# First mixer of a two-layer encoder: output products grouped by kind with the two heads alternating, and one diagonal product for both directions

## The chip, the core and the metric

The kernel runs on one core of one Trainium2 chip. Its time is device time in microseconds from the first to the last instruction with what lies around them, the median of three runs. The core has five engines with queues of their own: TensorE (PE in the profile, with PEld for its weight loads), VectorE (DVE), ScalarE (ACT), GpSimd (POOL) and SyncE (SP), which here issues DMAs. They wait for each other by semaphores.

## What is computed

An encoder trunk over 512 positions of 1024 channels: two mixers, each followed by a gated MLP with a width-3 convolution, and norms. The change lies in the first mixer, which holds four heads of gated linear attention (GLA) and four of HGRN2, all with 64 key and 128 value channels, forward and backward. Cut to that part, the reference is:

```python
def chunk_gated_scan(q, k, v, log_a, chunk):
    ...
    cum = jnp.cumsum(log_a, axis=3)
    rel = cum[:, :, :, :, None, :] - cum[:, :, :, None, :, :]
    decay = jnp.where(lower, jnp.exp(jnp.where(lower, rel, 0.0)), 0.0)
    scores = jnp.einsum('bhnid,bhnjd,bhnijd->bhnij', q, k, decay)
    o_intra = jnp.einsum('bhnij,bhnjv->bhniv', scores, v)
    ...                       # state carried from chunk to chunk
    o_inter = jnp.einsum('bhnid,bhndv->bhniv', q_in, prev)
    return (o_intra + o_inter).reshape(b, h, s, dv)

def bidir_scan(q, k_f, k_b, v, la_f, la_b, chunk):
    fwd = chunk_gated_scan(q, k_f, v, la_f, chunk)
    bwd = chunk_gated_scan(flip(q), flip(k_b), flip(v), flip(la_b), chunk)
    return fwd + flip(bwd)
```

A position meets itself in both directions with decay 1, so its diagonal score is q·k_f + q·k_b. In GLA both directions have the same k; in HGRN2 each has its own.

## The kernel before

The eight heads are worked in four pairs: 0 and 1 are GLA, 2 and 3 HGRN2. For pair p the tiles q, k and a (decays) hold head 0 in partitions 0 to 63 and head 1 in 64 to 127, the forward direction in columns 0 to 511 and the backward one behind it.

**Scores** (`scores`, from line 553). The scores inside a block of 128 positions are built over levels h = 1, 2, 4, ..., 64, and a first step h = 0 for the diagonal. `products(h)` issues small fp32 products in tile sc, a 64x64 quarter of TensorE's array each: head e chooses the rows of the array and one half of sc, position half b the columns. For h = 0 there are 32, both directions summed in place; ScalarE then copies the sum to s (L596). For h = 1 to 32 there are 32 each, of which VectorE takes what a mask allows into s (the mask copy, L610), for h = 64 there are 16, which ScalarE copies to A, the finished scores. Between levels VectorE multiplies decays into q and k (L602) and shrinks the decays (L606). A block of these products is a row of 32 or 64 records in the trace, since an fp32 product makes two records.

**Outputs** (`attend`, from line 639). TensorE transposes k (tile kT, copied by ScalarE, L654), multiplies it with v to the state changes dS, VectorE chains them to states Si (L666, L668), and TensorE forms the output of each head over four blocks J of 128 positions: A times v (kind A: 128 rows of the array), plus q times the state of each direction that has one (kind Q: 64 rows). The old order is head by head, block by block: A, Q; A, Q, Q; A, Q, Q; A, Q. Then each head is normalised (a square on ScalarE, a sum and a product on VectorE, a power on GpSimd), transposed (oT) and gated by the silu of p_g (L711).

**What fills TensorE between these**: the projections, which are 24 products of 512 columns each: p_q, p_k, p_hq, p_hz, v, the gates p_g0 to p_g7, and at the end wo. Their weights come by DMA and are split into two parts by ScalarE (L181) and VectorE (L183); a split waits until an older buffer of four is free.

**Order.** TensorE's order is set by a planner (class Sched): projections run as jobs in a list, and chains (scores, outputs) are resumed when a count of planned nanoseconds has passed. The count rises with each product by `cost` or by a formula on its size; the pauses stand in the table W (`lv0`, `o0` and so on). TensorE runs that order as it is; the orders of the other engines are made by a scheduler from it. PSUM tiles with tag hd have three buffers, which kT, dS and the outputs share.

Of the kernel before, what the change touches and what calls it, by code (L numbers as in the profile page):

```python
# [14 lines left out]
AF = mybir.ActivationFunctionType  # L15
ALU = mybir.AluOpType
PSUM = bass.MemoryType.PSUM

S = 512
# [116 lines left out]
class Net:  # L136
# [261 lines left out]
    def even(self):  # L398
# [16 lines left out]
        def et(shape, tag, name, bufs, dt=F32):  # L415
            return ep.tile(shape, dt, tag=tag, name=name, bufs=bufs)
# [4 lines left out]
        def hd_ps(shape, name):  # L421
            return pe.tile(shape, F32, tag="hd", name=name, bufs=3)
# [132 lines left out]
        def scores(p):  # L555
            yield (lambda: p < 2 or p - 2 in att), 0.0
            q, k, a = P[p]
            t = em.tile([128, S + 8], F32, tag=f"t{p % 2}", name=f"t{p}", bufs=1)
            s = et([128, 2, 256], f"s{p % 2}", f"s{p}", 1)
            s4 = s.rearrange("p e (J c) -> p e J c", c=64)  # L560
            A = et([128, 2, 4, 128], "A", f"A{p}", 2)

            def products(h):

                half = 256 * (next(turn) % 2)
                ps = two[:, :, half : half + 256].rearrange("p e (J c) -> p e J c", c=64)
                for J in range(4):
                    for d in range(2):  # L570
                        for b in range(2):
                            for e in range(2):
                                r = slice(64 * e, 64 * e + 64)
                                o = S * d + 128 * J + 64 * b
                                out = ps[64 * b : 64 * b + 64, e, J, :]
                                st, w = k[r, o : o + 64], q[r, o : o + 64]
                                if h == 64:
                                    if b == d:
                                        o += 64 - 128 * d
                                        self.mm(out, st, q[r, o : o + 64], cost=60)  # L580
                                elif h == 0:
                                    self.mm(out, st, w, d == 0, d == 1, cost=50)
                                else:
                                    half = lambda v: v.rearrange(
                                        "p (n two h) -> p n two h", two=2, h=h)[:, :, 1 - d, :]
                                    self.mm(half(out), st, half(w), cost=25)
                return ps

            psd = products(0)
            V.tensor_tensor(out=q, in0=q, in1=a[:, 0:S2], op=ALU.mult)  # L590
            T, h = a, 1
            while h <= 64:
                nb = S // h
                n = nb // 2
                if h == 1:
                    nc.scalar.activation(s, psd.rearrange("p e J c -> p e (J c)"), AF.Copy)  # L596
                yield W[f"lv{p}_0"] if h == 1 else W[f"lv{p}"]
                ps = products(h)
                for x, half, tt in (
                        (right_left(q, nb, h), right_left, left_right(T, nb, 1)),  # L600
                        (left_right(k, nb, h), left_right, right_left(T, nb, 1))):
                    V.tensor_tensor(  # L602
                        out=x, in0=x, in1=tt.to_broadcast([128, 2, n, h]), op=ALU.mult)
                nT = (t if h in (1, 4, 16) else a) if h < 64 else self.stile([128, 8], "t128", f"t128_{p}", 2)
                t2 = T[:, 0 : 4 * n].rearrange("p (n two) -> p n two", two=2)
                V.tensor_tensor(out=nT[:, 0 : 2 * n], in0=t2[:, :, 0], in1=t2[:, :, 1], op=ALU.mult)  # L606
                l, r = slice(0, 64), slice(64, 128)
                if h <= 32:
                    i = LV.index(h)
                    V.copy_predicated(  # L610
                        out=s4, mask=masks[:, i : i + 1, :].unsqueeze(1).to_broadcast([128, 2, 4, 64]),
                        data=ps)
                else:
                    nc.scalar.activation(A[l, :, :, r], ps[l], AF.Copy)
                    nc.scalar.activation(A[r, :, :, l], ps[r], AF.Copy)
                if h == 32:
                    nc.scalar.activation(A[l, :, :, l], s4[l], AF.Copy)
                    nc.scalar.activation(A[r, :, :, r], s4[r], AF.Copy)
                T = nT
                h *= 2  # L620
            AS[p] = (A, T)
            self.sch.chain(attend(p), W[f"at{p}"])
# [15 lines left out]
        def attend(p):  # L638
            g = p // 2
            yield (lambda: (g, 3) in VV), 0.0  # L640
            A, T = AS[p]
            Q, K = (dirs(x) for x in P[p][0:2])
            hv = [slice(128 * (u % 4), 128 * (u % 4) + 128) for u in (2 * p, 2 * p + 1)]
            heads = [slice(64 * e, 64 * e + 64) for e in range(2)]
            steps = ((0, 1, 2), (3, 2, 1))
            kTs, Sis = [], []
            for d in range(2):
                pk = hd_ps([128, 4, 128], f"kT{p}{d}")
                for J in steps[d]:
                    nc.tensor.transpose(pk[:, J, :], K[:, d, 128 * J : 128 * J + 128], self.ident)  # L650
                    self.sch.now += 107
                kT = et([128, 4, 128], "kT", f"kT{p}{d}", 2)
                c = slice(d, d + 3)
                nc.scalar.activation(kT[:, c], pk[:, c], AF.Copy)  # L654
                kTs.append(kT)
            yield W[f"dS{p}"]
            for d in range(2):
                dS = hd_ps([128, 4, 128], f"dS{p}{d}")
                for J in steps[d]:
                    for e in range(2):  # L660
                        self.mm(dS[heads[e], J, :], kTs[d][:, J, heads[e]], VV[g, J][:, hv[e]])

                Si = et([128, 4, 128], "Si", f"Si{p}{d}", 2)
                up = 1 - 2 * d
                c = steps[d][0]
                V.tensor_copy(Si[:, c + up, :], dS[:, c, :])  # L666
                for c in steps[d][1:]:
                    V.scalar_tensor_tensor(  # L668
                        out=Si[:, c + up, :], in0=Si[:, c, :], scalar=T[:, 4 * d + c : 4 * d + c + 1],
                        in1=dS[:, c, :], op0=ALU.mult, op1=ALU.add)  # L670
                Sis.append(Si)
            yield (lambda: p == 0 or (2 * p - 1 in fin and 2 * p - 2 in fin)), W[f"o{p}"]
            rest = []
            for e in range(2):
                u = 2 * p + e
                ps = hd_ps([128, 4, 128], f"o{u}")
                for J in range(4):
                    c = slice(128 * J, 128 * J + 128)
                    self.mm(ps[:, J, :], A[:, e, J, :], VV[g, J][:, hv[e]], True, False)
                    ds = [d for d in range(2) if J != 3 * d]  # L680
                    for d in ds:
                        self.mm(ps[:, J, :], Q[heads[e], d, c], Sis[d][heads[e], J, :], False, d == ds[-1])
                sq = self.actp.tile([128, 4, 128], F32, tag="nsq", name=f"osq{u}", bufs=2)
                nc.scalar.activation(sq, ps, AF.Square)
                ss = self.stile([128, 4], "ss", f"ss{u}", 2)
                V.tensor_reduce(out=ss, in_=sq, axis=mybir.AxisListType.X, op=ALU.add)
                col = self.rstd(ss, 128, 4, f"o{u}")
                o = et([128, 4, 128], "o", f"o{u}", 2)
                V.tensor_tensor(
                    out=o, in0=ps, in1=col.unsqueeze(2).to_broadcast([128, 4, 128]), op=ALU.mult)  # L690
                rest.append((u, o))
            att.add(p)
            for u, o in rest:
                yield W[f"cs{p}"]
                pt = sm_ps(f"oT{u}")
                for J in range(4):
                    nc.tensor.transpose(pt[:, 128 * J : 128 * J + 128], o[:, J, :], self.ident)
                    self.sch.now += 109
                o = o.rearrange("p a b -> p (a b)")
                if u not in RG:  # L700
                    nc.scalar.activation(o, pt, AF.Copy)
                    pt = o
                O[u] = (pt, o)
                finish(u)
# [902 lines left out]
```

## Time and profile before

| | |
|---|---|
| median of three runs | 1289.49 us (1288.77 to 1289.98) |
| profiled execution: its own time | 1288.18 us |
| its span, first to last instruction | 1286.2 us |
| TensorE, matmuls busy | 1258.7 us (98%) |
| VectorE busy | 836.5 us (65%) |
| ScalarE busy | 489.9 us (38%) |
| GpSimd busy | 189.8 us (15%) |
| mean granted TensorE clock | 0.993 of full speed |

Busy times are sums over the whole span. A matmul's record lasts longer than its share of the array, since the next one begins before it ends; the distance from start to start is what it costs. Times in rows count from the span's start.

### The profile page before, as it was taken

Reading aid. Unit: us, or ns where it says so; the run is one execution under the profiler, and the core shown is the slowest. Engines: PE = TensorE matmul, PEld = TensorE weight load, DVE = VectorE, ACT = ScalarE, POOL = GpSimd, SP = SyncE. Lnnn points to the kernel's source line nnn. Section 1 sums busy time; section 2 is a strip of 40 time slices with the busy share of each in tenths; the row PEclk is TensorE's granted clock in tenths of the full one; section 3 lists DMA queues with packets and bytes.
Section 4 is the critical chain, followed back from the end, with each engine's and each line's share of the span. In section 5 each row is a group of like instructions: output and inputs, shape, how many; then the busy total and the mean of one; then the engine's idle time right before and its main releaser. Section 6 shows DMA issues by size and latency. Waiting matters only on the chain. (4 is left out here: it accounts for less than half of the span.)

```text
span 1286.2 us, 19499 instructions
## 1 busy us (share of the span) xinstructions
PE 1258.7 (98%) x7863; PEld 1038.7 (81%) x7863; DVE 836.5 (65%) x1317; ACT 489.9 (38%) x657; POOL 189.8 (15%) x283
## 2 busy tenths in 40 slices
PE   7989999999999999999999999999999999999997
PEld 5767887888888888888888889788888888888887
DVE  6665277656999478637665885775577637755753
ACT  4523344333443244324442324333444314433442
POOL 2000000024008526230021330001200000000012
PEclk8999999999999999999999999999999999999999
DMA  7111321132332534333246532423232322233211
GB/s 227 55 51 50 108 83 58 51 99 99 99 99 69 168 102 129 115 124 110 87 160 227 175 100 76 148 82 99 99 99 99 98 96 91 85 106 98 90 58 67
DMA packets 53819, 132.95 MB, mean 103 GB/s; under 512 B 12193, under 2 KB 17505, under 8 KB 53729
## 3 DMA queue, kind: packets, MB, share of 16 engines
q1 hardware_dynamic: 53008, 131.15, 31.6%
q8 instruction: 62, 1.02, 0.3%
q10 hardware_dynamic: 720, 0.55, 0.1%
q14 instruction: 29, 0.23, 0.1%
HBM read 120.14 MB, written 11.53 MB: 102 GB/s over the span
## 5 line engine op out<-in xcount | busy, mean ns | idle before, releaser
L191 PE MATMUL pu<-xh_f,h_u 128*128 128x512 f32 x704 | 275.6, 392 | 0.0
L191 PE MATMUL pu<-xh_f,l_u 128*128 128x512 f32 x704 | 274.1, 389 | 0.0
L191 PE MATMUL pu<-xl_f,h_u 128*128 128x512 f32 x704 | 274.0, 389 | 0.0
L191 PEld LDWEIGHTS pu<-xh_f,l_u 128*128 128x128 f32 x704 | 132.2, 188 | 27.8
L191 PEld LDWEIGHTS pu<-xh_f,h_u 128*128 128x128 f32 x704 | 132.1, 188 | 27.2
L191 PEld LDWEIGHTS pu<-xl_f,h_u 128*128 128x128 f32 x704 | 132.2, 188 | 26.9
L181 ACT ACTIVATE h_u<-r_u 128x1024 fp32r<-128x1024 f32 x88 | 93.2, 1059 | 129.9 <-PE pd L191 59.9
L312 DVE SCALAR_TENSOR_TENSOR c<-upad,convp,c 128x512 f32<-128x512 f32 x176 | 135.6, 772 | 3.6 <-ACT c L309 1.0
L191 PE MATMUL pd<-gh,h_d 128*128 128x512 f32 x331 | 129.3, 391 | 0.1
L191 PE MATMUL pd<-gl,h_d 128*128 128x512 f32 x331 | 128.9, 389 | 0.2 <-DVE gl L323 0.2
L191 PE MATMUL pd<-gh,l_d 128*128 128x512 f32 x331 | 128.8, 389 | 0.0
L183 DVE TENSOR_TENSOR l_u<-r_u,h_u 128x1024 fp32r<-128x1024 f32 x88 | 108.8, 1236 | 14.6 <-ACT h_u L181 13.9
L305 DVE TENSOR_TENSOR upad<-pu,rstd_f 128x512 f32<-128x512 f32 x88 | 60.5, 689 | 72.2 <-PE pu L191 70.4
L345 DVE TENSOR_TENSOR x<-pd,x 128x512 f32<-128x512 f32 x45 | 31.0, 690 | 102.4 <-PE pd L191 102.4
L309 ACT ACTIVATE c<-upad,convp 128x512 f32<-128x512 f32 x88 | 71.3, 812 | 22.4 <-DVE upad L305 19.1
L181 ACT ACTIVATE h_d<-r_d 128x896 fp32r<-128x896 f32 (+1 forms) x48 | 47.2, 988 | 71.1 <-PE pd L191 39.4
L191 PEld LDWEIGHTS pd<-gl,h_d 128*128 128x128 f32 x331 | 62.2, 188 | 13.3 <-DVE gl L323 0.5
L191 PEld LDWEIGHTS pd<-gh,h_d 128*128 128x128 f32 x331 | 62.1, 188 | 13.2 <-ACT gh L322 0.5
L191 PEld LDWEIGHTS pd<-gh,l_d 128*128 128x128 f32 x331 | 62.1, 188 | 13.0
L322 ACT ACTIVATE gh<-g 128x512 fp32r<-128x512 f32 x44 | 27.8, 631 | 116.8 <-DVE g L319 116.8
L183 DVE TENSOR_TENSOR l_d<-r_d,h_d 128x896 fp32r<-128x896 f32 (+1 forms) x48 | 55.2, 1152 | 5.6 <-ACT h_d L181 3.3
L317 ACT ACTIVATE sa<-c 128x512 f32<-128x512 f32 x44 | 27.8, 632 | 80.8 <-DVE c L312 80.8
(407 smaller groups left out, 2313.0 us busy)
## 6 DMA issues: line engine op xcount, KB each, us to landing
r_u<-in_w_up SPq DMA_DIRECT2D x88, 512.0 KB, 3.7
r_d<-in_w_down SPq DMA_DIRECT2D x32, 448.0 KB, 3.3
r_wo<-in_w_out SPq DMA_DIRECT2D x16, 512.0 KB, 3.6
r_d<-in_w_down SPq DMA_DIRECT2D x16, 512.0 KB, 3.6
w<-dw SPq DMA_DIRECT2D x20, 256.0 KB, 4.4
r_v<-in_we_v SPq DMA_DIRECT2D x8, 512.0 KB, 3.7
r_g<-in_we_g SPq DMA_DIRECT2D x8, 512.0 KB, 3.8
r_ov<-in_wo_v SPq DMA_DIRECT2D x8, 384.0 KB, 3.1
```

The source lines that it names most:

```text
L181: nc.scalar.activation(hi[:, 0:n], raw[:, 0:n], AF.Copy)
L183: eng.tensor_tensor(out=lo[:, 0:n], in0=raw[:, 0:n], in1=hi[:, 0:n].bitcast(F32), op=ALU.subtract)
L191: self.nc.tensor.matmul(ps, a, b, start=start, stop=stop)
L305: nc.vector.tensor_tensor(out=u[:, 1 : S + 1], in0=pss[half], in1=self.rbc, op=ALU.mult)
L309: nc.scalar.activation(c, u[:, 1 : S + 1], AF.Identity, scale=cw[:, 1:2], bias=cw[:, 3:4])
L312: nc.vector.scalar_tensor_tensor(out=c, in0=u[:, o : o + S], scalar=cw[:, tap : tap + 1], in1=c, op0=ALU.mult, op1=ALU.add)
L317: nc.scalar.activation(sa, cs[0], AF.Silu)
L322: nc.scalar.activation(h, g, AF.Copy)
L345: nc.vector.tensor_tensor(out=x[k], in0=ps, in1=x[k], op=ALU.add)
```

## The change

In `products(0)` only the products of one direction stay. For pairs 0 and 1, whose k is the same in both directions, ScalarE's copy of the diagonal doubles them. For pairs 2 and 3 VectorE first adds the two directions of k into a new tile ks (named k0 in the code), from which the products read. The planned cost of the diagonal falls from 32 x 50 to 16 x 30.

The output products of a pair are issued in another order: first the eight of kind A, four blocks of head 0 and four of head 1; then the twelve of kind Q, the two heads in turn. Both heads' PSUM tiles are taken at once, and the normalisation of both heads follows all products.

```diff
-                                if h == 64:
+                                if h == 0:
+                                    if d == 0:
+                                        self.mm(out, k0[r, o : o + 64], w, cost=30)
+                                elif h == 64:
                                     if b == d:
                                         o += 64 - 128 * d
                                         self.mm(out, st, q[r, o : o + 64], cost=60)
-                                elif h == 0:
-                                    self.mm(out, st, w, d == 0, d == 1, cost=50)
...
+            k0 = k
+            if p >= 2:
+                k0 = et([128, S], "e", f"ks{p}", 2)
+                V.tensor_tensor(out=k0, in0=k[:, 0:S], in1=k[:, S:S2], op=ALU.add)
             psd = products(0)
...
-                    nc.scalar.activation(s, psd.rearrange("p e J c -> p e (J c)"), AF.Copy)
+                    nc.scalar.activation(s, psd.rearrange("p e J c -> p e (J c)"), AF.Copy,
+                                         scale=2.0 if p < 2 else 1.0)
...
+            pss = [hd_ps([128, 4, 128], f"o{2 * p + e}") for e in range(2)]
             for e in range(2):
-                u = 2 * p + e
-                ps = hd_ps([128, 4, 128], f"o{u}")
                 for J in range(4):
-                    c = slice(128 * J, 128 * J + 128)
-                    self.mm(ps[:, J, :], A[:, e, J, :], VV[g, J][:, hv[e]], True, False)
-                    ds = [d for d in range(2) if J != 3 * d]
-                    for d in ds:
-                        self.mm(ps[:, J, :], Q[heads[e], d, c], Sis[d][heads[e], J, :], False, d == ds[-1])
+                    self.mm(pss[e][:, J, :], A[:, e, J, :], VV[g, J][:, hv[e]], J == 0, False)
+            for J in range(4):
+                c = slice(128 * J, 128 * J + 128)
+                ds = [d for d in range(2) if J != 3 * d]
+                for d in ds:
+                    for e in range(2):
+                        self.mm(pss[e][:, J, :], Q[heads[e], d, c], Sis[d][heads[e], J, :],
+                                False, J == 3)
+            for e in range(2):
+                u, ps = 2 * p + e, pss[e]
```

On TensorE the outputs of pair 0 (heads 0 and 1, tiles o0 and o1) begin before with:

```order
L191 MATMUL o0_1144<-v0_0_696,A0_430 128x128
L191 MATMUL o0_1144<-Si01_1095,q0_316 128x128
L191 MATMUL o0_1144<-v0_1_795,A0_430 128x128
L191 MATMUL o0_1144<-Si00_1084,q0_316 128x128
L191 MATMUL o0_1144<-Si01_1095,q0_316 128x128
L191 MATMUL o0_1144<-v0_2_932,A0_430 128x128
```

and now, from the third product of head 0 on:

```order
L191 MATMUL o0_1115<-v0_2_862,A0_430 128x128
L191 MATMUL o0_1115<-v0_3_1021,A0_430 128x128
L191 MATMUL o1_1116<-v0_0_628,A0_430 128x128
L191 MATMUL o1_1116<-v0_1_763,A0_430 128x128
L191 MATMUL o1_1116<-v0_2_862,A0_430 128x128
L191 MATMUL o1_1116<-v0_3_1021,A0_430 128x128
L191 MATMUL o0_1115<-Si01_1066,q0_316 128x128
L191 MATMUL o1_1116<-Si01_1066,q0_316 128x128
L191 MATMUL o0_1115<-Si00_1055,q0_316 128x128
L191 MATMUL o1_1116<-Si00_1055,q0_316 128x128
```

The kinds no longer alternate, and neighbours of kind Q belong to different heads.

Also on TensorE, where pair 3 (q3, k3) begins and pair 2 (q2, k2) has its last level, among the projections of gate p_g4, the order before was:

```order
L191 MATMUL p_g4_2064<-xh_m03_180,l_g4_1803 128x512
L191 MATMUL sc_237<-q3_1903,k3_1904 64x64 x32
L191 MATMUL sc_237<-q2_1566,k2_1567 64x64 x16
L191 MATMUL p_g4_2064<-xh_m04_184,h_g4_1802 128x512
L191 MATMUL p_g4_2064<-xl_m04_185,h_g4_1802 128x512
```

and now it is:

```order
L191 MATMUL p_g4_2018<-xh_m03_180,l_g4_1757 128x512
L191 MATMUL sc_237<-q3_1857,ks3_2072 64x64 x16
L191 MATMUL p_g4_2018<-xh_m04_184,h_g4_1756 128x512
L191 MATMUL p_g4_2018<-xl_m04_185,h_g4_1756 128x512
L191 MATMUL p_g4_2018<-xh_m04_184,l_g4_1757 128x512
L191 MATMUL p_g4_2018<-xh_m05_188,h_g4_1756 128x512
L191 MATMUL p_g4_2018<-xl_m05_189,h_g4_1756 128x512
L191 MATMUL p_g4_2018<-xh_m05_188,l_g4_1757 128x512
L191 MATMUL sc_237<-q2_1534,k2_1535 64x64 x16
```

Pair 3's diagonal has half its products and reads the sum ks3, and six projections stand between the two blocks.

On ScalarE, where it copies pair 2's transposed k (kT20, kT21), the order before was:

```order
L614 ACTIVATE A2_1676<-sc_237 64x8x64
L615 ACTIVATE A2_1676<-sc_237 64x8x64
L654 ACTIVATE kT20_2187<-kT20_2183 128x384
L654 ACTIVATE kT21_2193<-kT21_2189 128x384
L181 ACTIVATE h_wo0_0_2261<-r_wo0_0_2259 128x1024
L711 ACT_TABLE_LOAD
L711 ACTIVATE r4_2256<-r4_2256 128x512
```

and now it is (line numbers below the change are shifted):

```order
L621 ACTIVATE A2_1644<-sc_237 64x8x64
L622 ACTIVATE A2_1644<-sc_237 64x8x64
L181 ACTIVATE h_wo0_0_2179<-r_wo0_0_2177 128x1024
L722 ACT_TABLE_LOAD
L722 ACTIVATE r4_2174<-r4_2174 128x512
L661 ACTIVATE kT20_2166<-kT20_2162 128x384
L661 ACTIVATE kT21_2172<-kT21_2168 128x384
```

The copies of kT moved behind the weight split of wo, a table load and the silu of gate 4.

## Rows read from the trace of the kernel before

**Rows 1.** Page, first part: busy us, share of span, instructions by engine.

```profile
PE 1258.7 (98%) x7863; PEld 1038.7 (81%) x7863; DVE 836.5 (65%) x1317; ACT 489.9 (38%) x657; POOL 189.8 (15%) x283
```

**Rows 2.** Stretches: us, busy by engine in page order, granted clock, DMA; the first mixer.

```profile
38.00:280.00 242.00, 235.58 (x2898) 187.58 (x2897) 142.78 (x238) 85.63 (x119) 9.08 (x16) 0.99 0.20 63
```

**Rows 3.** Waits of TensorE: waiter, awaited, us in total, times, longest.

```profile
PE sc L191 <- DVE s L610: 2.9, 3, 1.3
...
PE sc L191 <- DVE a L606: 2.0, 1, 2.0
...
PE sc L191 <- ACT s L596: 1.4, 2, 0.7
```

**Rows 4.** Timeline of TensorE (start us, us): groups of pair 0's outputs.

```profile
99.17 0.49 PE L191 MATMUL o<-Si,q 64*128 64x128 f32 x2
99.58 0.49 PE L191 MATMUL o<-v,A 128*128 128x128 f32 x2
100.00 0.71 PE L191 MATMUL o<-Si,q 64*128 64x128 f32 x4
100.64 0.49 PE L191 MATMUL o<-v,A 128*128 128x128 f32 x2
```

**Rows 5.** Stretches of the four output stages, tile o alone: their sum and mean.

```profile
sum 29.92, PE 29.91 PEld 22.17 DVE 3.46 ACT 2.75; mean PE 7.48 PEld 5.54 DVE 0.86 ACT 0.69
```

**Rows 6.** Timeline of TensorE: pair 0's dS and what follows.

```profile
93.92 1.53 PE L191 MATMUL dS<-v,kT 128*64 128x128 f32 x24
95.39 0.50 PE L191 MATMUL p_g<-xh_m,h_g 128*128 128x512 f32 x1
```

**Rows 7.** Stretches, tile sc alone: a diagonal and a level 64.

```profile
42.41:43.50 1.09, 1.09 (x64) 1.02 (x64) 0.00 (x0) 0.00 (x0) 1.00 0.00 0
...
87.72:88.34 0.62, 0.62 (x32) 0.56 (x32) 0.00 (x0) 0.00 (x0) 1.00 0.00 0
```

**Rows 8.** Groups of TensorE in the first of these: count, busy us, mean ns.

```profile
L191 PE MATMUL sc<-q,k 64*64 64x64 f32 x64 | 1.2, 221 | 0.0
```

**Rows 9.** Timeline of TensorE: score products, in brackets the idle time before.

```profile
66.33 1.14 PE L191 MATMUL sc<-q,k 64*64 64x32 f32 x64 [1.15 <-DVE s L610]
...
74.89 1.14 PE L191 MATMUL sc<-q,k 64*64 64x32 f32 x64 [2.05 <-DVE a L606]
...
84.37 1.14 PE L191 MATMUL sc<-q,k 64*64 64x32 f32 x64 [0.46 <-DVE s L610]
...
206.87 1.16 PE L191 MATMUL sc<-q,k 64*64 64x64 f32 x64 [1.33 <-DVE s L610]
...
225.03 1.14 PE L191 MATMUL sc<-q,k 64*64 64x32 f32 x64
```

**Rows 10.** Stretch behind the longest of these waits (columns as rows 2).

```profile
75.00:80.20 5.20, 5.20 (x76) 4.26 (x77) 2.19 (x5) 0.00 (x0) 0.00 (x0) 0.67 0.00 0
```

**Rows 11.** Timeline of VectorE: mask copies, and a product of 512 columns.

```profile
206.01 0.71 DVE L610 COPY_PREDICATED s<-masks,sc 128x512 f32<-128x512 int32 x1
206.62 0.67 DVE L606 TENSOR_TENSOR t<-a 128x512 f32<-128x512 f32 x1
...
220.03 0.72 DVE L610 COPY_PREDICATED s<-masks,sc 128x512 f32<-128x512 int32 x1
```

**Rows 12.** Timeline of ScalarE around pair 2's copies of transposed k.

```profile
212.07 0.87 ACT L654 ACTIVATE kT<-kT 128x384 f32<-128x384 f32 x2 [1.38 <-PE kT L650]
215.63 1.06 ACT L181 ACTIVATE h_wo<-r_wo 128x1024 fp32r<-128x1024 f32 x1 [2.69 <-issue]
216.71 1.28 ACT L711 ACT_TABLE_LOAD   x1
218.00 0.63 ACT L711 ACTIVATE r<-r 128x512 f32<-128x512 f32 x1
```

**Rows 13.** Timeline of TensorE: first products of the MLP behind the mixer.

```profile
301.95 0.39 PE L191 MATMUL pu<-xh_f,h_u 128*128 128x512 f32 x1
302.18 0.39 PE L191 MATMUL pu<-xl_f,h_u 128*128 128x512 f32 x1
```

## The prediction, made before the changed kernel ran

> **What bounds the kernel now.** I read the page's busy times first: TensorE runs matmuls in 98% of the span, VectorE is busy in 65% [rows 1]. The table by stretches then says whether that holds where the change is made: from 38 to 280 us, the first mixer after its start, matmuls fill 235.6 of 242 us at full clock, VectorE 142.8, ScalarE 85.6 [rows 2]. So TensorE's queue sets the end here; a microsecond of its own work taken away is a microsecond of the kernel, unless a wait takes its place. Last, the list of waits: its three entries for the score products (tile sc) are the only waits of TensorE inside this stretch that are worth naming, 2.9 + 2.0 + 1.4 = 6.3 us [rows 3]. They are the places where other engines are nearly late already, and a faster TensorE arrives there sooner.
>
> **Term 1, the output products.** A pair of heads has 20 fp32 products, each two records in the trace: 8 of kind A (128 rows of the array) and 12 of kind Q times state (64 rows). In the old order the kinds alternate. The timeline shows what that costs: a group of four Q records runs from 100.00 to the next group at 100.64, a group of two from 99.17 to 99.58 [rows 4]. Two more records take 0.23 us, so 0.11 each; the rest of a group, 0.41 - 0.22 = 0.19, call it 0.2 us, comes with the change of kind. There are 16 groups in a pair's stage: 40 x 0.11 + 16 x 0.2 = 7.6 us, against 7.48 measured in the mean of four stages [rows 5]. The new order has two changes of kind (A to Q, Q to what follows). Its 16 A records take 16 x 0.11 = 1.76 us.
>
> The 24 Q records now alternate between head 0 (rows 0 to 63 of the array) and head 1 (rows 64 to 127). No row of the old output stage shows that pair. The nearest are two others. The dS products alternate between two halves of the columns: 24 records of the same length need 1.47 us with everything, that is 12 steps of 0.11 and the change [rows 6]. The diagonal score products use four quarters, rows and columns both: 64 records of 221 ns each fit in 1.2 us of busy time [rows 7, 8], which two halves of the columns alone would not give. So halves of the rows overlap too, and I take 12 steps: 12 x 0.11 = 1.32 us. Together 1.76 + 1.32 + 2 x 0.2 = 3.48; the model overshoots the old stage by 0.1, so 3.4. Saved: 7.48 - 3.4 = 4.08 a pair, **16.3 us** for four. If the halves do not overlap, the stage has 12 more steps, 3.4 + 1.3 = 4.7, and four pairs save 11.1.
>
> The overlap rests on the score products writing their heads to different halves of tile sc; the new products do the like, each head into a tile of its own. The Trainium skill, "TensorEngine Tiling (Array Packing)", Gotcha 1: PSUM Pressure, says that row tiles write to different PSUM banks and can't access one bank at the same time. By that rule the overlap would be lost, and 11.1 us saved in place of 16.3, if both tiles lay in one bank; the quarters' pace in sc, whose heads lie apart, agrees with it. What it would do is the first rival.
>
> **Term 2, the diagonal.** Only half of the 32 products stay. The table by stretches has both sizes: 32 products (64 records) take 1.09 us, 16 (32 records, level 64) 0.62 [rows 7]. 0.47 x 4 = **1.9 us** saved. The factor 2 in ScalarE's copy is free. For pairs 2 and 3 an addition of 512 columns is new on VectorE; a product of that size took 0.67 us [rows 11]. It stands before the score products, so it counts in term 4.
>
> **Term 3, new neighbours.** The cost numbers that the planner adds up fall by 1120 a pair, so what follows moves by a few products. Before, three places had two blocks of score products, or a block and dS, side by side and shared a change of kind; nearly all now stand alone. Two or three more changes of 0.2: **+0.5 us**.
>
> **Term 4, waits.** This is where gain is given back. A block of score products waits until the mask copy of the block before it is done. The price depends on what lies between: nothing 2.05 us, three products 1.15, six 0.46 [rows 9]. By the order of the changed kernel, pairs 0 and 1 now have one block with nothing ahead (q0 level 32, q1 level 4: 2.05), one with three (1.15), one with six (0.46), and a last with three after level 64, taken at 0.8 between 0.46 and 1.15. Sum 4.46, against 0.7 + 1.15 + 2.05 + 0.46 = 4.36 before (0.7 is one of the two waits for ScalarE [rows 3]): +0.1. In pairs 2 and 3 the diagonal of pair 3 waited 1.33 for the mask copy that starts at 206.01 [rows 9, 11], and level 64 behind it 0.7, the other wait for ScalarE [rows 3]. On VectorE the addition now follows that copy, so the first is 1.33 + 0.67 = 2.0, and six products stand before level 64, so the second goes: 0.
>
> New waits, each with its bound:
> - pair 2, dS on the copy of transposed k: on ScalarE the copy now stands behind a weight copy, a table load and the silu, 1.06 + 1.28 + 0.63 = 2.97 [rows 12], plus half of the 0.87 copy, 3.4 from the end of p_g4. TensorE has a block of score products (1.1), six transposes of 0.11 (0.7) and three products of 0.23 with a change of kind (0.9) till then [rows 4, 13], 2.7: the difference is 0.7, taken at 0.8 for the second change; 0 to 1.2.
> - pair 3, level 4 after the outputs: the mask copy ended at 220.75, the products came at 225.03 [rows 11, 9]: 4.3 us of slack, and the output stage that filled it loses 4.1. The state updates of dS now come just ahead on VectorE too. 0 to 1.5, taken at 1.0.
> - pair 1, dS: both heads' normalisation now begins after all products, so ScalarE and VectorE do in a row what they did under the second head's 3.7 us. 0 to 1.9, taken at 1.2, a third of that cover.
> - pair 0, dS (transposes now 3 products ahead, two copies of A just before): 0 to 1, taken at 0.5.
> - pair 2, diagonal behind the addition: 0 to 0.67, taken at 0.5.
> - pair 3, transposes behind VectorE's gate product and weight split, which now stand ahead of the last k update: 0 to 1.5, taken at 0.8.
> Sum 0.1 + 0.8 + 1.0 + 1.2 + 0.5 + 0.5 + 0.8 = **+4.9 us**, bounds +0.1 and about +8.
>
> **Term 5, the clock.** After the 2.05 us wait the granted clock of 75.0 to 80.2 is 0.67 [rows 10]: two thirds of those 5.2 us at 1.2 instead of 2.4 GHz, half of that time lost, 1.7 us. The same wait stays. The 2.0 us wait at pair 3 is nearly as long; 1.33 and 0.7 with a block between were followed by no fall. A chance of one in four: **+0.4**.
>
> **Sum.** -16.3 - 1.9 + 0.5 + 4.9 + 0.4 = -12.4 us. Against the profiled execution's 1288.18 that is 1275.8; the median of the three runs is 1.3 above it, so 1289.49 - 12.4 = **1277.1 us**, -1.0%. Behind the mixer TensorE's order is the same, and it stays bound by its queue, so the gain lasts to the end.
>
> **Rivals.**
> - *The two heads don't overlap* (passes of one head run out before the other's start): +1.3 x 4 = 5.3, 1282.4. Against it the quarters' pace; chance 7%.
> - *The waits don't grow*, since the engines behind catch up: without 4.9 and 0.4, 1271.8. For it: VectorE is idle in 99 of 242 us. Against: the orders on its queues. 12%.
> - *The waits reach their bounds and the clock falls twice more*: 3.1 + 3.4 - 0.4, about 6 us more, 1283. 14%.
> - *Slower*: after every new and old wait the clock falls as after 2.05 us. Eleven waits x 1.7 = 18.7 less the 0.4, 1295. It takes more than nine falls to pass +0.2%. Against: of the old waits only the longest had one. 2%.
> - *The mixer's end is set elsewhere* (weights arriving, VectorE), so the change does nothing that can be seen: 1288 to 1289. Against: matmuls fill 97% of the stretch. 3%.
>
> The forecast itself has 62%, three us to either side. A measurement of this kernel tells about 0.2% from no change, 2.6 us. Faster by more than that: all but the last two, 95%; within it 3%; slower 2%. The range: 1272.0 leaves out the lower half of the second rival (6%), 1283.0 takes in the first and leaves out half of the third (7%) and the last two (5%).
>
> **What would show it.** The four output stages at 3.3 to 3.5 us each with 24 Q records in steps of 0.11 (4.7 if the heads don't overlap); the diagonals at 0.62; waits of sc, dS and the transposes near 11 us in sum in place of 6.3; one or two stretches at half clock; the first product of the next layer (pu) some 12 us before its old 301.95 [rows 13]. Wrong would be an output stage above 4 us, waits above 15 us, or a gain in the mixer that is gone at the end.

## The result, and the profile after

The changed kernel takes 1276.07 us (median of four runs, 1275.27 to 1278.2) beside 1289.63 us for the kernel before (median of four, 1288.77 to 1289.98): a ratio of 0.9898 with a 95% interval of 0.9881 to 0.9916, 13.6 us less. The prediction was 1277.1 us, with a range of 1272.0 to 1283.0. The profiled execution of the changed kernel took 1278.2 us, 10.0 less than the profiled one of the kernel before; where the other 3.6 us are is told below, under term 5. One execution of a later kernel, `outputs_only`, took 2082.6 us at a mean granted clock of 0.554 and is left out of that kernel's median.

The page's first part answers to [rows 1]. TensorE has 128 matmul records fewer (four diagonals of 32) and is still busy in 98% of the span:

```profile
PE 1245.1 (98%) x7735; PEld 1029.2 (81%) x7735; DVE 838.9 (66%) x1319; ACT 488.8 (38%) x657; POOL 190.6 (15%) x283
```

The stretches of the four output stages, tile o alone (one of them and the sum), answer to [rows 5]: 13.66 us where 29.92 stood, 3.41 a stage in place of 7.48.

```profile
97.07:100.48 3.41, 3.41 (x40) 3.17 (x39) 0.00 (x0) 0.00 (x0) 1.00 0.00 0
...
sum 13.66, PE 13.65 PEld 12.68 DVE 0.69 ACT 0.36; mean PE 3.41 PEld 3.17 DVE 0.17 ACT 0.09
```

The timeline of pair 0's outputs answers to [rows 4]: two groups where sixteen stood. 24 Q records run from 98.95 to the next block at 100.48 (that row is part of one, and its end doesn't matter here): 1.53 us, which is 12 steps of 0.11 and one change of kind.

```profile
97.07 1.95 PE L191 MATMUL o<-v,A 128*128 128x128 f32 x16
98.95 1.61 PE L191 MATMUL o<-Si,q 64*128 64x128 f32 x24
100.48 0.73 PE L191 MATMUL sc<-q,k 64*64 64x32 f32 x36
```

The four diagonals, tile sc alone, answer to [rows 7]: 0.62 us each.

```profile
sum 2.50, PE 2.50 PEld 2.22 DVE 0.00 ACT 0.00; mean PE 0.62 PEld 0.55 DVE 0.00 ACT 0.00
```

The list of TensorE's waits in the first mixer answers to [rows 3]: 10.8 us where 6.3 stood. Line numbers are shifted by the change: L617 is the mask copy, L594 the new addition, L661 ScalarE's copy of transposed k, L622 its copy of level 64, L609 VectorE's products that set q and k for the next level.

```profile
PE sc L191 <- DVE s L617: 5.9, 5, 2.0
PE sc L191 <- DVE ks L594: 1.9, 1, 1.9
PE dS L191 <- ACT kT L661: 1.8, 2, 0.9
PE sc L191 <- ACT A L622: 0.7, 1, 0.7
PE kT L657 <- DVE k L609: 0.5, 1, 0.5
```

And the timeline of TensorE says where each stands (blocks that waited; the idle time in brackets); it answers to [rows 9]:

```profile
62.13 1.14 PE L191 MATMUL sc<-q,k 64*64 64x32 f32 x64 [0.47 <-DVE s L617]
...
72.66 1.14 PE L191 MATMUL sc<-q,k 64*64 64x32 f32 x64 [1.16 <-DVE s L617]
...
81.22 1.14 PE L191 MATMUL sc<-q,k 64*64 64x32 f32 x64 [2.05 <-DVE s L617]
...
88.21 1.14 PE L191 MATMUL sc<-q,k 64*64 64x32 f32 x64 [0.71 <-ACT A L622]
...
107.70 0.69 PE L191 MATMUL sc<-q,k 64*64 64x64 f32 x32 [0.42 <-DVE s L617]
...
114.68 1.53 PE L191 MATMUL dS<-v,kT 128*64 128x128 f32 x24 [0.91 <-ACT kT L661]
...
197.96 0.69 PE L191 MATMUL sc<-q,ks 64*64 64x64 f32 x32 [1.91 <-DVE ks L594]
...
207.36 1.53 PE L191 MATMUL dS<-v,kT 128*64 128x128 f32 x24 [0.86 <-ACT kT L661]
...
221.31 1.14 PE L191 MATMUL sc<-q,k 64*64 64x32 f32 x64 [1.78 <-DVE s L617]
```

The granted clock (stretches of the changed kernel, columns as in [rows 2]) answers to [rows 10]. Behind the wait of 2.05 us, which ends at 81.22, it stays at 1.00, where it had fallen before. Behind the waits of 1.91 and 1.78 us it falls to its lower level, 1.2 GHz, with 0.57 in the mean of four us each: 4 x 0.43 = 1.7 us lost at each.

```profile
81.00:86.00 5.00, 4.78 (x83) 3.86 (x87) 3.73 (x7) 3.38 (x4) 0.00 (x0) 1.00 0.02 5
199.00:203.00 4.00, 4.00 (x41) 2.86 (x40) 1.81 (x3) 1.17 (x3) 0.00 (x0) 0.57 0.02 4
223.00:227.00 4.00, 4.00 (x13) 3.11 (x12) 2.68 (x6) 0.00 (x0) 0.00 (x0) 0.57 0.45 134
725.00:732.00 7.00, 6.21 (x30) 6.21 (x31) 1.85 (x4) 0.00 (x0) 0.00 (x0) 0.52 0.36 109
```

The last row lies in the second mixer, at a wait of 2.6 us (to 725.79) that stands in both kernels: the fall begins while TensorE still waits. In the profiled execution before the clock fell there too, but only behind the wait (to 737.02) and for a shorter time:

```profile
738.00:742.00 4.00, 4.00 (x24) 4.00 (x23) 0.11 (x2) 0.00 (x0) 0.00 (x0) 0.58 0.29 99
```

The first product of the next layer, which answers to [rows 13], starts 11.3 us before its old 301.95:

```profile
290.63 0.39 PE L191 MATMUL pu<-xh_f,h_u 128*128 128x512 f32 x1
```

These 11.3 us add up from the rows: 16.3 (outputs) and 1.9 (diagonals) saved; 4.5 more in waits (10.8 - 6.3) and 1.7 more for the clock (two falls in place of one) given back: 12.0. The 0.7 left over is put down to the new neighbours, estimated at 0.5; no run measures them apart. Between the mixers nothing changes: the same products start 11.3 us before their old places up to the second mixer's wait. There 1.2 us go with the longer fall of the clock, and 10.0 are left at the end of this execution.

### The profile page after: what moved, and what is told of

Its sections match the earlier page's. It is cut to its first block, busy times and chain, and to the rows that moved or that the text cites. A ratio compares the mean times of both kernels' runs of the same rounds, so it can differ in the third digit from the quotient of the medians.

```text
span 1276.3 us, 19254 instructions
## 1 busy us (share of the span) xinstructions
PE 1245.1 (98%) x7735; PEld 1029.2 (81%) x7735; DVE 838.9 (66%) x1319; ACT 488.8 (38%) x657; POOL 190.6 (15%) x283
```

## Experiments

The questions: do the two heads overlap in the Q products, or did fewer changes of kind bring all of the gain; what is the diagonal's part worth; and are the waits that ate a quarter of the gain a price of the change or of the order?

### Heads overlap or not

`q_by_head`: the changed kernel, with Q products head by head.

```diff
-            for J in range(4):
-                c = slice(128 * J, 128 * J + 128)
-                ds = [d for d in range(2) if J != 3 * d]
-                for d in ds:
-                    for e in range(2):
+            for e in range(2):
+                for J in range(4):
+                    c = slice(128 * J, 128 * J + 128)
+                    ds = [d for d in range(2) if J != 3 * d]
+                    for d in ds:
                         self.mm(pss[e][:, J, :], Q[heads[e], d, c], Sis[d][heads[e], J, :],
                                 False, J == 3)
```

> The changed kernel with one thing other: the twelve Q products of a pair stand head by head (six of head 0, then six of head 1), not in turn. Kinds are still grouped, so the changes of kind are as few. My theory: neighbours on different halves of the array's rows overlap, and without that 12 more steps of 0.11 are paid: output stages of 3.41 + 1.3 = 4.7 us, +5.2 us in sum, of which the waits that lie right behind the output stages (pair 1 dS 0.9, pair 3 level 4 1.8) give back up to 2: 1279 to 1281. Rival: all of the stage's gain comes from fewer changes of kind, and the two heads in turn give nothing: stages of 3.4 us and 1276.

Measured: 1279.59 us (ratio 0.9923, interval 0.9910 to 0.9937), 3.5 above the changed kernel's median. All four output stages take 4.41 us. The timeline of pair 0's:

```profile
98.23 1.95 PE L191 MATMUL o<-v,A 128*128 128x128 f32 x16
100.10 2.60 PE L191 MATMUL o<-Si,q 64*128 64x128 f32 x24
102.64 1.08 PE L191 MATMUL sc<-q,k 64*64 64x32 f32 x60
```

The A products take what they took; the Q products take 2.54 us from start to start in place of 1.53. So the alternation is worth 1.0 us a stage, and the rival (nothing from the overlap) falls. It isn't the 1.3 that were expected: nine steps of 0.11 are lost, not twelve. Something overlaps even here, and the only place where the halves of the rows meet is where head 0 ends and head 1 begins. The next run looks there.

`q_by_block`: the same two loops the other way round inside a block of 128 positions, so that a head has two or four records in a row before it is the other's turn.

```diff
-                for d in ds:
-                    for e in range(2):
+                for e in range(2):
+                    for d in ds:
                         self.mm(pss[e][:, J, :], Q[heads[e], d, c], Sis[d][heads[e], J, :],
                                 False, J == 3)
```

> The changed kernel with the Q products in groups: for each block first those of head 0, then those of head 1 (2 or 4 records of one head in a row), not strictly in turn. With all six of one head ahead of the other's, the stage took 4.41 us and not 4.75, since head 1 began beside the last four records of head 0. My theory: TensorE looks a few records ahead for rows that are free, so groups of up to four records still overlap nearly fully: stage 3.4 to 3.6 us. Rival: only direct neighbours overlap; with groups of four about a third of the overlap is lost: 3.9 us or more.

Measured: 3.51 to 3.52 us in each of the four stages, one execution at 1275.8 us.

```profile
97.61:101.13 3.52, 3.52 (x40) 3.27 (x39) 0.00 (x0) 0.00 (x1) 1.00 0.00 0
```

Strict turns aren't needed. Groups of up to four records cost one step of 0.11 more than strict alternation, where the rival (only direct neighbours overlap) asked for 3.9 us or more. So records overlap that don't stand next to each other: a record of one head begins while earlier ones of the other still queue.

`kinds_mixed`: overlap kept, changes of kind put back. For each block the two A products, then its Q products with the heads in turn: 8 changes in a pair in place of 2.

```diff
-            for e in range(2):
-                for J in range(4):
-                    self.mm(pss[e][:, J, :], A[:, e, J, :], VV[g, J][:, hv[e]], J == 0, False)
             for J in range(4):
                 c = slice(128 * J, 128 * J + 128)
                 ds = [d for d in range(2) if J != 3 * d]
+                for e in range(2):
+                    self.mm(pss[e][:, J, :], A[:, e, J, :], VV[g, J][:, hv[e]], J == 0, False)
                 for d in ds:
```

> The changed kernel with the output products of a pair ordered block by block: for each of the four blocks the two A products, then its Q products, heads in turn. The heads overlap as in the changed kernel, but the kind changes 8 times in a pair in place of 2. My theory: a change of kind costs 0.19 us whatever stands around it, so the stage is 3.41 + 6 x 0.19 = 4.55 us. Rival: the gain of the change comes from the overlap of the heads alone, and the changes cost little once both heads' products stand between them: 3.5 to 3.8 us.

Measured, tile o alone in pair 0's stage: 4.60 us (the other three 4.59), and 1279.94 us for the one execution.

```profile
98.36:102.96 4.60, 4.59 (x40) 3.62 (x39) 0.00 (x0) 0.00 (x0) 1.00 0.00 0
```

(4.60 - 3.41) / 6 = 0.20 us for a change of kind, as the prediction had it from [rows 4]. Neighbours write to different tiles here, so the price goes with the kind and not with a sum that two neighbours share. The two halves of term 1 are thus measured apart, and they add up: 14 changes of 0.2 are 2.8, 12 steps of 0.11 are 1.3 (nine of them seen in `q_by_head`, where three still overlap), together 4.1 beside the 4.07 saved in a stage.

### What the diagonal is worth

`outputs_only` has the regrouped outputs and the old diagonal, `diagonal_only` the new diagonal and the old outputs. The edit of the first, against the changed kernel (cut: the addition and the factor 2 in ScalarE's copy are gone as well):

```diff
-                                if h == 0:
-                                    if d == 0:
-                                        self.mm(out, k0[r, o : o + 64], w, cost=30)
-                                elif h == 64:
+                                if h == 64:
                                     if b == d:
                                         o += 64 - 128 * d
                                         self.mm(out, st, q[r, o : o + 64], cost=60)
+                                elif h == 0:
+                                    self.mm(out, st, w, d == 0, d == 1, cost=50)
```

> Only the output products are regrouped; the diagonal is that of the kernel before (32 products, planned at 50 each, no addition for pairs 2 and 3). The question is what the diagonal's part of the change is worth. My theory: the four output stages take 3.41 us each as in the changed kernel (16.3 us saved), the diagonals are back at 1.09 us, and since the planned counts are those of before, the score waits of pairs 0 and 1 (4.4 us in sum), and those of pair 3's diagonal and pair 2's level 64 (1.33 + 0.7) are as before; new waits come only behind the shorter output stages (pair 1 dS about 1, pair 3 level 4 and level 8 about 1.5 in sum). Waits about 9 us in place of 10.8, so the diagonal's 1.9 us are lost again by its own waits: 1289.6 - 16.3 + 2.7 = 1276, the time of the whole change. Rival: the diagonal's 1.9 us are a gain of their own and the waits don't depend on it: 1278.

Measured: 1276.63 us (ratio 0.9901, interval 0.9886 to 0.9916), as good as the whole change; the interval takes in the rival's 1278 as well, which `diagonal_only` below decides. The trace comes from another execution of it, `outputs_again` (one run, 1276.9 us).

> The regrouped outputs with the old diagonal once more, for its trace. My theory: output stages 3.41 us, diagonals 1.09; waits: score products of pairs 0 and 1 4.4 us as in the kernel before, pair 3's diagonal and pair 2's level 64 1.3 + 0.7 as before, and new ones only behind the shorter output stages: dS of pair 1 about 1.4, pair 3's last levels about 1.5 to 2. Rival: the waits of the whole change (10.8 us) stand here too.

TensorE's waits in that trace, 9.9 us in sum:

```profile
PE sc L191 <- DVE s L611: 5.1, 5, 1.8
PE sc L191 <- DVE a L607: 2.0, 1, 2.0
PE sc L191 <- ACT s L597: 1.4, 2, 0.7
PE dS L191 <- ACT kT L655: 1.4, 1, 1.4
```

Against the kernel before only dS of pair 1 (1.4) and two blocks behind shorter output stages (1.8 and 0.4) are new. So the faster outputs alone bring 3.6 us of waits.

`diagonal_only` is the other half of the diff.

> Only the diagonal is changed (16 products, doubled in ScalarE's copy for pairs 0 and 1, VectorE's addition for pairs 2 and 3, planned cost 30); the output products stand head by head as before. My theory: 1.9 us saved on the diagonals, 0.5 for new neighbours, pair 3's diagonal waits 1.9 (1.33 and 0.7 before), dS of pair 2 0.8, transposes of pair 3 0.5, the clock as before: the sum is -1.9 + 0.5 + 1.3 = about 0, 1289 to 1290. Rival: the order that the planner makes of it costs nothing and the diagonals' 1.9 us are saved: 1287.7.

Measured: 1288.23 us (eleven runs), ratio 0.9996 with an interval of 0.9987 to 1.0005: no gain, and the rival's 1.9 us (a ratio of 0.9985) lie just outside. Its diagonals take 0.62 us, 1.9 saved in sum. TensorE's waits come to 7.7 us, some 1.3 more than before:

```profile
PE sc L191 <- DVE s L616: 3.7, 3, 2.0
PE sc L191 <- DVE ks L593: 1.9, 1, 1.9
PE dS L191 <- ACT kT L660: 0.9, 1, 0.9
PE sc L191 <- ACT A L621: 0.7, 1, 0.7
PE kT L656 <- DVE k L608: 0.5, 1, 0.5
```

With 0.5 for new neighbours, an estimate, the 1.9 us are used up. The saving is there, and waits take it back. Not all of them come from the planner's order: pair 3's diagonal waits 0.58 us longer (1.91 beside 1.33) because VectorE's addition now stands ahead of it.

### Waits of the work, or of the order

The diagonal's new planned cost lowers the planner's count by 1120 a pair, and all that follows moves. `old_count` leaves the work and undoes that.

```diff
-                                        self.mm(out, k0[r, o : o + 64], w, cost=30)
+                                        self.mm(out, k0[r, o : o + 64], w, cost=100)
```

> The changed kernel with one number other: the planned cost of a diagonal product is 100 in place of 30, so that 16 of them add up to the 1600 of the 32 before and the planner resumes its chains at the products where it did before the change. My theory: the waits of the diagonal part come from the moved order, not from less work; with the old counts pair 2's dS and pair 3's transposes no longer wait (1.4 us less), pairs 0 and 1 keep their 4.4 us, and the diagonals stay at 0.62: about 1275. Rival: the waits come from the work that is gone (TensorE arrives sooner wherever the blocks stand), and the time is that of the change, 1276.

Measured: 1275.37 us (1273.06 to 1278.63), which the spread doesn't tell from the changed kernel. The two waits named did go (dS of pair 2, transposes of pair 3), but dS of pair 1 waits 1.4 in place of 0.9 and pair 2's level 64 waits 0.7 again; the sum is 10.5 us. Theory and rival stay undecided by this run: an old table is no better a place for the blocks than a table that moved by accident.

So the next kernels moved the blocks on purpose. `three_numbers` is `old_count` with three pauses set anew (of the table's lines only the entries that differ are shown, here and below):

```diff
-    "lv0": 3800.0, "dS1": 100.0, "sc3": 3350.0,
+    "lv0": 4490.0, "dS1": 1480.0, "sc3": 2660.0,
```

> The changed kernel with the diagonal's planned cost at 100 and three pauses set anew: lv0 4490 (before 3800), dS1 1480 (100), sc3 2660 (3350). My theory: pair 1's two blocks no longer stand side by side with pair 0's, so the 2.05 us wait goes, and dS of pair 1 stands behind more projections, so its 1.4 us goes; pair 3's diagonal still waits 1.9 or more. Waits about 7 us in place of 10.8: 1271.5 to 1273. Rival: as above, 1275.

Measured: 1269.31 us (ratio 0.9855, interval 0.9841 to 0.9868), below the 1271.5 to 1273 that were expected. The waits come to 6.5 us, near the expected 7, but in the traced execution the clock falls once in the first mixer (behind the wait of 2.6 us) and not at all in the second; the waits of 2.05 us and of dS are gone, and pair 3's diagonal, which the third number brings forward, waits longer:

```profile
PE sc L191 <- DVE s L617: 3.9, 4, 1.8
PE sc L191 <- DVE ks L594: 2.6, 1, 2.6
```

`tuned` has 17 pauses set anew, on top of the planned cost of 100 (the two runs above and this one differ in the table alone):

```diff
-    "at0": 2500, "at1": 3645, "at2": 1800, "cs3": 5150, "dS0": 550, "dS1": 100, "dS2": 500,
-    "lv0": 3800, "lv0_0": 3000, "lv2": 3300, "lv2_0": 3000, "lv3_0": 3000,
-    "o0": 2175, "o2": 1000, "o3": 1000, "sc0": 6050, "sc3": 3350,
+    "at0": 2730, "at1": 4795, "at2": 3180, "cs3": 3770, "dS0": 780, "dS1": 1480, "dS2": 845,
+    "lv0": 4720, "lv0_0": 2425, "lv2": 2955, "lv2_0": 2310, "lv3_0": 2310,
+    "o0": 1945, "o2": 540, "o3": 0, "sc0": 6395, "sc3": 2660,
```

> The changed kernel with the diagonal's planned cost at 100 and 17 pauses in the planner's table set anew (lv0 4720, lv0_0 2425, lv2 2955, lv2_0 2310, lv3_0 2310, dS0 780, dS1 1480, dS2 845, sc0 6395, sc3 2660, at0 2730, at1 4795, at2 3180, o0 1945, o2 540, o3 0, cs3 3770); no work is added or taken away. The blocks of score products, of dS and of transposes are spread so that three to six projections stand between a block and the copy that it waits for. My theory: what is left of the change's gain is lost in waits (10.8 us) and in the clock that falls after the longest of them; with the blocks spread the waits of TensorE in the first mixer come to 3 to 5 us, none above 1.8, and at most one stretch at half clock stands there: 1276.1 - 6.5 - 1 = 1268 to 1270. Rival: the waits only move, since VectorE and ScalarE have no more time than before: 1273 to 1277.

Measured: 1264.19 us (1263.43 to 1265.03), ratio 0.9812 with an interval of 0.9798 to 0.9825. It is the fastest of all, 24 us below the kernel before in the same comparison (1288.27), and 4 to 6 us below what was expected: waits of 2.3 us are left where 3 to 5 had been expected,

```profile
PE sc L191 <- DVE s L617: 1.6, 2, 1.3
PE sc L191 <- ACT kT L661: 0.7, 1, 0.7
```

and the granted clock of the mixer is 1.00 throughout, where a fall had been allowed for:

```profile
38.00:256.00 218.00, 215.70 (x2768) 174.96 (x2767) 142.14 (x240) 84.49 (x119) 9.69 (x16) 1.00 0.21 70
```

8.5 us of waits (10.8 - 2.3), 3.4 for the two falls of the clock in the first mixer and 1.2 for the longer one in the second (here it is 1.7 us again) are 13.1; the profiled executions of the changed kernel and of this one are 1278.2 - 1264.99 = 13.2 us apart, the medians 11.9 (11.1 by their ratios to the kernel before). The rival (waits only move) falls: VectorE does the same work here (838.2 us busy beside 838.9), only TensorE's blocks stand elsewhere.

`before_tuned` gives the kernel before the same table.

> The kernel before with the same table of pauses as the tuned one; outputs and diagonals are those of before. My theory: its own waits of 6.3 us come down to about 2, one clock fall fewer, so it gains 4 to 5 us (1284 to 1285), and the tuned changed kernel stands 16 to 17 us below it: the change's own work, 16.3 on the outputs and 1.9 on the diagonals less 0.5 for the kinds and 1 for waits. Rival: the table helps both kernels alike only by what the change had brought in, and the kernel before stays at 1288 to 1290.

Measured: 1286.42 us (eleven runs), ratio 0.9985 with an interval of 0.9976 to 0.9994. The waits came down to 1.1 us as the theory had it, but the gain was 1.9 us and not 4 to 5. The trace shows why. In pair 3's output stage, still in the old order, TensorE waits once for a state:

```profile
247.79 0.48 PE L191 MATMUL o<-Si,q 64*128 64x128 f32 x2 [0.87 <-DVE Si L668]
```

and some 2.9 us later the clock falls and stays down for over 10 us, though TensorE is busy all the time:

```profile
250.00:261.00 11.00, 11.00 (x35) 8.14 (x34) 2.48 (x6) 1.19 (x2) 2.01 (x2) 0.53 0.27 96
```

11 x 0.47 = 5.2 us, in the one execution that was traced. So 5.2 less in waits, 1.7 less for the fall that this trace no longer has at 75, 5.2 more here: 1.7 in sum, and 1.9 measured. The two tuned kernels are 22.2 us apart: 16.3 + 1.9 for the work, less 1.2 for waits (2.3 beside 1.1), and 5.2 for this fall make 22.2, without anything for neighbours; 16 to 17 had been expected, without this fall.

### The clock, from execution to execution

> The changed kernel, unchanged, in another execution: do TensorE's waits and the stretches at half clock lie where they lay? My theory: the waits are set by the order and come again within 0.1 us, while the clock falls after some of the waits of 1.8 to 2.6 us and not after others, another choice in each execution, so that the executions of one kernel spread over about 3 us with a mean granted clock between 0.989 and 0.994. Rival: the falls belong to the places (after the diagonal of pair 3 and the level behind pair 2's outputs, not after the 2.05 us wait of pair 1), and the trace repeats the first.

Measured: 1276.47 us (1275.74 to 1277.84); the waits of the trace are those of the first within 0.01 us. Its clock:

```profile
82.00:86.00 4.00, 4.00 (x28) 3.20 (x22) 2.99 (x4) 1.41 (x2) 0.00 (x0) 0.57 0.03 6
199.00:204.00 5.00, 4.60 (x88) 3.41 (x89) 3.44 (x6) 3.00 (x6) 0.00 (x0) 1.00 0.01 3
222.00:226.00 4.00, 4.00 (x40) 3.36 (x33) 3.63 (x6) 0.59 (x1) 0.00 (x0) 0.57 0.41 128
```

Now it falls behind the 2.05 us wait (which ends at 81.11 here), and not behind the 1.9 us wait at pair 3's diagonal: the other way round than in the first trace, with the same kernel and the same waits. The rival (falls belong to places) is out. Over all traces with these waits the clock fell behind the 2.05 us wait in 3 of 9, behind the 1.9 us wait in 3 of 7, behind pair 3's level 8 (1.7 to 1.8 us) in 2 of 7, behind the 2.6 us wait of the second mixer in 9 of 12, and behind the 2.6 us wait that `three_numbers` has at pair 3's diagonal in its one trace. It fell behind none of the 16 waits of 1.1 to 1.5 us in these first mixers.

## Why the prediction was right, point by point

**Bound.** Right: TensorE's queue set the end, and the 11.3 us that the mixer saved arrived at the end, less what the clock took.

**Term 1.** Right in sum and in both halves: 3.41 us a stage beside 3.4, 16.3 us in sum. That the quarters' pace of the score products carries over to halves of the rows was the one thing that no row showed; it holds. The rival without overlap had a size a little too large (4.7 us a stage; 4.41 measured), since the heads overlap at their boundary even in that order. The Trainium skill, "TensorEngine Tiling (Array Packing)", Gotcha 1: PSUM Pressure, says that different row tiles can't access the same PSUM bank at the same time. The runs agree so far as the two heads' tiles lie in different banks and overlap; both heads in one bank wasn't tried.

**Term 2.** Right: 0.62 us each. That it would be given back in full isn't said there: the diagonal alone gains nothing.

**Term 3.** 0.5 estimated; the remainder of the sum is 0.7.

**Term 4.** The sum was right, 11.2 us expected (6.3 and 4.9 more; 11.3 by the places below) and 10.8 measured, but not each part. In us, place by place:

| place | predicted | measured |
|---|---|---|
| pairs 0 and 1, four blocks | 4.46 | 4.39 (0.47 + 1.16 + 2.05 + 0.71) |
| pair 1, level 64 | - | 0.42 |
| pair 0, dS | 0.5 | 0 |
| pair 1, dS | 1.2 | 0.91 |
| pair 2, diagonal | 0.5 | 0 |
| pair 3, diagonal | 2.0 | 1.91 |
| pair 2, dS | 0.8 | 0.86 |
| pair 3, level 4 | 1.0 | 0 |
| pair 3, level 8 | - | 1.78 |
| pair 3, transposes | 0.8 | 0.5 |

What was worked out from rows and the order together came within 0.1: the blocks of pairs 0 and 1, pair 3's diagonal (the mask copy, then the addition), pair 2's dS behind the weight split, the table load and the silu. What was taken from within a range without such a working came smaller or not at all: pair 1's dS 0.91 of 1.2, pair 3's transposes 0.5 of 0.8, pair 0's dS and pair 2's diagonal not. Pair 1's level 64 was named nowhere. And one step named the wrong block: pair 3's level 4, right behind the outputs at 214.10, waits for nothing; the next block, level 8, waits 1.78 us. The timeline of VectorE shows the queue ahead of the copy that it waits for:

```profile
214.83 1.28 DVE L697 TENSOR_REDUCE ss<-osq 128x4 f32<-128x512 f32 x2 [2.69 <-ACT osq L695]
...
217.68 0.69 DVE L700 TENSOR_TENSOR o<-o,ncol_o 128x512 f32<-128x512 f32 x1 [0.90 <-POOL ncol_o L251]
...
219.94 0.69 DVE L700 TENSOR_TENSOR o<-o,ncol_o 128x512 f32<-128x512 f32 x1 [0.90 <-POOL ncol_o L251]
220.54 0.72 DVE L617 COPY_PREDICATED s<-masks,sc 128x512 f32<-128x512 int32 x1
```

Both heads' normalisation stands between the outputs and level 4's mask copy at 220.54, and VectorE waits 0.90 us in it twice for GpSimd's power. In the kernel before the same copy was the last before that block as well, and it was just in time (VectorE, and TensorE's next block, of which the row shows the start):

```profile
229.35 0.74 DVE L610 COPY_PREDICATED s<-masks,sc 128x512 f32<-128x512 int32 x1
...
230.42 0.79 PE L191 MATMUL sc<-q,k 64*64 64x32 f32 x40
```

The copy ended at 230.09, and level 8 began at 230.42. The prediction had followed the block behind the outputs and its slack of 4.3 us, and not the next one, whose slack was 0.3. So the mistake was to look at the first user only; that the sum held is in part luck, since errors of some 2 us either way cancel.

**Term 5.** Undersized. It had one fall that stays and a second with a chance of one in four; the profiled execution has two in the first mixer at 1.7 us each, the price that [rows 10] gave. One is behind the wait at pair 3's diagonal, which the prediction had given its chance; the other is behind pair 3's level 8, which it didn't name, and the fall behind 2.05 us, which it had taken as certain, didn't come. What was wrong is the picture: a fall isn't a property of the 2.05 us wait, but something that may or may not follow each of the waits near 2 us. This is also where the profiled executions and the medians part: the mean granted clock of the four first runs is 0.990, 0.991, 0.993 and 0.992 at 1278.2, 1276.77, 1275.36 and 1275.27 us, and the profiled one was the slowest, 2.1 above the median. The profiled execution of the kernel before was 1.5 below its median (1288.18 beside 1289.63). So the 12.4 us of the forecast stand between the 10.0 of the profiled executions and the 13.6 of the medians, and how near the number came owes something to the clock of these executions.

**Rivals.** No overlap: out by `q_by_head`. Waits don't grow, or reach their bounds: they came to 10.8, near the forecast. Slower, or an end set elsewhere: the interval (0.9881 to 0.9916) leaves both out.

## What to carry to other kernels

Group small products by the part of the array that they use, and let neighbours use different halves of its rows: here each avoided change is worth 0.2 us, and the overlap 1.0 to 1.3 of a stage that then takes 3.4. After a stage has been made shorter, set the order around it anew: the change alone brought 13.6 us, 18 us of work saved, and with blocks moved away from the copies they wait for it brought 24; the same new order gave the old kernel 1.9. When a stage shrinks, follow not only the first block behind it but each that reads what the stage's epilogue has queued on other engines.

## What the runs showed of the hardware

- TensorE's clock may fall to 1.2 GHz after waits near 2 us and may not: the same kernel with the same waits fell in one execution behind the wait of 1.91 us and not behind that of 2.05, in another the other way round. Each fall of the first mixer in these two traces cost 1.7 us; the longer one of the second mixer (725 to 732), which began within the wait, cost 1.2 us more than the one in the kernel before. A kernel without such waits in its first mixer spread over 1.6 us in five runs, the changed kernel over 2.9 and 2.1 in four each. The Trainium skill, "TensorE: Matmul & The Clock Gate", Part 1, tells that the number of products at half clock at a kernel's start differs from execution to execution; the runs here show the like in the middle of one.
- A long wait isn't needed. In `before_tuned` the clock fell after a wait of 0.87 us within output products of alternating kinds, and stayed low for over 10 us of work; the mean granted clock of its eleven runs is 0.989 or 0.990, which would fit such a fall in each, but only one was traced. The same stage without that wait kept its clock in the kernel before ([rows 5] lie at full pace). Which of the two, wait or alternation, the chip answers to wasn't tried apart.
- Records on different halves of the array's rows overlap over a distance: in `q_by_block` groups of up to four records of one head cost 0.1 us a stage more than strict turns (3.52 beside 3.41).
